# Seven quarter-product units of the second feed-forward layer placed anew, and the mLSTM's head steps later in TensorE's order

## The chip, the cores and the metric

One core of one Trainium2 chip runs the whole program. The metric is the device time of one execution in microseconds (us), the median of several runs. The core's engines are PE (TensorE, matmuls), DVE (VectorE), ACT (ScalarE), POOL (GpSimd) and SP (SyncE, which here only issues DMAs). Each has its own list of instructions, taken in order, and they wait for each other through semaphores.

## The reference, cut to what matters

Two layers over x of 256 positions by 2048 channels, float32. Layer 0 is pooling and attention, layer 1 an mLSTM, and behind each comes a gated MLP with 5632 hidden channels:

```python
for layer in range(DEPTH):
    h = rms_norm(x, norm_mix[layer])
    if layer % 2 == 0:
        ...  # pooling, attention, output projection
    else:
        mixed = mlstm_mixer(h, w_in_c[o], b_gate_c[o], h_norm_c[o], w_out_c[o])
    x = x + mixed
    x = x + conv_ffn(rms_norm(x, norm_ffn[layer]), w_up[layer], conv_w[layer], conv_b[layer], w_down[layer])
def conv_ffn(x, w_up, conv_w, conv_b, w_down):
    u = x @ w_up
    ...  # u: width-3 convolution over positions
    gate, val = jnp.split(u, 2, axis=-1)
    return (jax.nn.silu(gate) * val) @ w_down
```

The mLSTM has 8 heads of 256 channels: per head a 256 by 256 score matrix with a mask, exponential weights and a normaliser for each of the two directions, times the values; then a per-head norm, times a sigmoid gate, and an output projection.

## The kernel before, in words

**Weights.** All weights pass through one stream (class Stream) of chunks of 128 by 1024 numbers, 512 KB each. SP issues a chunk's load into one of 7 buffers w (8 in the feed-forward layers), ACT copies it rounded into the first half of a buffer hl (L167), DVE writes the remainder into its second half (L168), so that three passes of TensorE (high times high, high times low, low times high) stand for one exact product. There are 5 buffers hl (6 in the feed-forward layers), so ACT and DVE work at most that many chunks ahead of PE. PE, whose program order is written out by hand, reads a chunk in 12 matmuls of 512 columns (names mv, mo, op, dn), or 16 of 512 and 256 columns by turns (mq, mk, up).

**The feed-forward layer.** The hidden channels are 44 row tiles of 128, gate and value together, in six chunks of 4, 8, 8, 8, 8 and 8 (FCH, L33). A tile is either plain (function up, name up) or one of four that a unit makes. A unit (quads, names p1, p4, p5, p6) multiplies the four quadrants of two row blocks and two column blocks with seven products in place of eight. That takes sums of the weight quadrants. They are made beforehand and lie in DRAM, named G, one for each of a unit's eight pairs of blocks. When a unit's products are done, DVE adds them up into tiles c, PE turns these round (name tr, in finish, L1110), and ACT and DVE make the convolution, the SiLU and the product (tail), which end in g. The function down (dn) then multiplies g with the down weights, in the order of row tiles that DORDER (L34) gives. PE's interleaving is laid down by the table UNITS (L1272), each entry of which is (chunk, half of the chunk, first and last slot, kind), and by _ffn_plan (L1279), which deals the units' steps into slots between plain tiles and down products. Kind 1 reads three sums of a pair from DRAM, kind 2 reads two and lets DVE add the third as the chunk passes by (L155).

**How the sums are made.** A table (places, L1462 to L1468) gives for each pair the chunk of the stream at whose load its steps are issued. Written (at, 5) they go by DMA in four steps 5 loads apart: SP copies parts of the weights from DRAM to DRAM and POOL adds other parts to them with accumulating DMAs (L139, L143). Written (at, 1, 6) they go by DVE: SP loads the pair's 1 MB into a buffer in SBUF called a room (gb or gm, L120), DVE makes four additions of 128 by 512 (L124 to L127), and SP stores the result (L129). Rooms are handed out in the order of st.rooms (L772).

**The mLSTM.** For each pair of heads PE multiplies values (mv), then for each head queries and keys (mq, mk, 64 matmuls each), then the output gate of the pair (mo, 96 matmuls). Each head also runs a chain of small steps: qk (PE), the weighting and the matrix A (DVE), its transpose atr (PE), a copy and remainder at (ACT, DVE), the product with the values av (PE), a norm whose power -0.5 is taken on POOL (ry_h, L303), and, with the gate og (ACT and DVE, whose reciprocals stand at L923), the transpose htr (PE). These steps are generators in a list (class Weave). Each yields a delay in PE's microseconds, and the next one's PE instructions are put into PE's order when that many have been emitted. For PE's order the delays are thus the only thing that matters. DVE's, ACT's and SP's order is set by a scheduler that works on estimates of its own.

Of the kernel before, what the change touches and what calls it, by code (L numbers as in the profile page):

```python
# [32 lines left out]
FCH = [4, 8, 8, 8, 8, 8]  # L33
DORDER = ((0, 1), (0, 1, 3, 2), (2, 3, 0, 1), (0, 1, 3, 2), (0, 1, 3, 2), (0, 1, 3, 2))  # L34
CH = 8
# [213 lines left out]
def trunk(ctx: ExitStack, tc: tile.TileContext, gx, xT, xn, call, catt, cml, weights, make, out):  # L249
# [22 lines left out]
    st = Stream(tc, wp, sp, made, weights, make, 5, 2)  # L272
# [14 lines left out]
    wv = Weave()  # L287
# [473 lines left out]
    def mlstm_layer(norm, nxt):  # L761
        with ExitStack() as es:
# [7 lines left out]
            gm = kp.tile([P, 2048], F32, tag="gm", name="gm")  # L770
            gb = actp.tile([P, 2, 2048], F32, tag="B1", name="gb")
            st.rooms = ([gb[:, 0], gb[:, 1], gm] * 7)[:20] + [gm] * 8  # L772

# [13 lines left out]
            def gates(ps):  # L787
# [34 lines left out]
                a.dma_start(gd, gr)  # L822
                yield 16.0
                cols = psp.tile([P, 2, 2, 40], F32, tag="ps", name="cols")
                n = 0
# [28 lines left out]
            def head(h, q, kk, vt, hh):  # L854
# [10 lines left out]
                a.activation(arg, arg, AF.Exp)  # L865
                yield 5.5
                qk = psp.tile([P, 2, S], F32, tag="ps", name=f"qk{h}")
# [7 lines left out]
                for i, (t, d, c, n, o) in enumerate(blocks):  # L875
# [11 lines left out]
                                       ALU.mult, ALU.add)  # L887
                yield 5.0
                tr = psp.tile([P, 2, S], F32, tag="ps", name=f"atr{h}")
# [5 lines left out]
                v.tensor_sub(at[:, 1], tr, at[:, 0].bitcast(F32))  # L895
                yield 3.2
                av = psp.tile([P, 2, MD], F32, tag="ps", name=f"av{h}")
# [12 lines left out]
                for t in range(2):  # L910
                    a.activation(hn[:, t, :], av[:, t, :], AF.Copy, scale=r[:, t : t + 1])
                hns[h] = hn

            def gated(ps, heads):
                og = t1p.tile([P, 2, len(heads) * MD], F32, tag="og", name=f"og{heads[0]}")
                for t in range(2):
                    a.activation(og[:, t, :], ps[:, t, :], AF.Exp, scale=nrcol[:, t : t + 1])
                yield 1.2
                for i, h in enumerate(heads):
                    o = og[:, :, i * MD : i * MD + MD]  # L920
                    v.tensor_scalar_add(o, o, 1.0)
# [50 lines left out]
    def ffn_layer(layer, norm, nxt):  # L972
        with ExitStack() as es:
# [79 lines left out]
            def quads(fs, c, i0, name, apart):  # L1053
# [34 lines left out]
                for p in range(m):  # L1088
# [9 lines left out]
                    if p % 2:  # L1098
# [53 lines left out]
            def down(c, gt, b):  # L1152
                kts = [2 * k + j for k in DORDER[c] for j in range(2)]
                last = c == len(FCH) - 1
# [108 lines left out]
def _down_chunks(w):  # L1263
    out, k0 = [], 0
    for n in FCH:
# [10 lines left out]
)  # L1276


def _ffn_plan(layer):  # L1279

    slots = []
    for c, n in enumerate(FCH):
        fill = [("n", c, i) for i in range(n) if not any(u[0] == c and u[1] == i // 4 for u in UNITS[layer])]
        if c:
            per = len(fill) // NB
            fill = sum(([*fill[per * b : per * b + per], ("d", c - 1, b)] for b in range(NB)), [])
            if c == 2 and any(u[:2] == (1, 1) for u in UNITS[layer]):
                fill = [fill[i] for i in ((0, 2, 1, 4, 3, 6, 5, 7), (0, 1, 3, 2, 5, 7, 4, 6))[len(UNITS[layer]) > 6]]
            if c > 3 and len(UNITS[layer]) > 5:
                fill.sort(key=lambda e: e[0] == "d")  # L1290
        for e in fill:
# [31 lines left out]
def _ffn_order(layer, up, dn, four, last):  # L1323
# [4 lines left out]
    for step in _ffn_plan(layer):  # L1328
# [5 lines left out]
        elif kind == "d":  # L1334
            seq.append(dn[d0[c] + i * (FCH[c] // 2) + DORDER[c][n]])
        else:
# [141 lines left out]
```

## Time and profile before

| | us |
|---|---|
| median of 3 runs | 2164.73 (2164.2 to 2165.07) |
| the profiled execution, whole | 2164.91 |
| its span, first to last instruction | 2163.1 |
| PE busy | 2147.9 |
| DVE busy | 1798.1 |
| ACT busy | 1334.9 |
| POOL busy | 237.3 |

Layer 1's mLSTM lies between about 967 and 1454 us of the span, its feed-forward layer from there to the end. A matmul's duration in the profile holds its way through the array, so that those that follow each other overlap: PE counts as busy from a matmul's start until its modelled end, and only what is left beyond that shows as a wait.

### The profile page before, as it was taken

What the parts mean: (1) busy time and instruction counts of PE and PEld (TensorE: products, weight loads), DVE (VectorE), ACT (ScalarE), POOL (GpSimd) and SP (SyncE); (2) the same over time, 40 slices, a digit from 0 to 9 for tenths busy, and PEclk for the clock granted to TensorE, in tenths of its full rate; (3) what the DMA queues carried; (4) which work ended last, traced back from release to release, by engine and by line L of the source; (5) the groups of instructions that cost most, each with busy time, mean ns of one, the idle gap of its engine ahead of it and who ended that gap; (6) DMA issues with size and microseconds to landing.
All of it is one profiled execution on the core that took longest, in us unless ns stands there. A gap on an engine that the chain in (4) does not pass through costs nothing.

```text
span 2163.1 us, 30963 instructions
## 1 busy us (share of the span) xinstructions
PE 2147.9 (99%) x10752; PEld 1815.6 (84%) x10752; DVE 1798.1 (83%) x2522; ACT 1334.9 (62%) x1872; POOL 237.3 (11%) x296
## 2 busy tenths in 40 slices
PE   9999999999999999999999999999999999999999
PEld 7888888888888888888788888888888887888887
DVE  7686698989889888868888877769898888988985
ACT  7665566766557565755444544456685776766853
POOL 0222111111111111100000000000111111110000
PEclk9999999999999999999999999999999999999999
DMA  9889889999999999969898977778999999998882
GB/s 351 257 226 254 257 255 353 304 341 316 310 336 303 350 306 363 319 187 311 326 361 320 347 253 275 273 267 228 339 336 342 349 319 350 347 317 300 279 269 98
DMA packets 212768, 648.59 MB, mean 300 GB/s; under 512 B 26394, under 2 KB 28738, under 8 KB 205442
## 3 DMA queue, kind: packets, MB, share of 16 engines
q1 hardware_dynamic: 181216, 593.30, 76.4%
q0 software_dynamic: 28320, 49.56, 14.5%
q10 hardware_dynamic: 3074, 3.75, 0.8%
q8 instruction: 84, 1.38, 0.2%
q14 instruction: 74, 0.61, 0.1%
HBM read 615.00 MB, written 130.07 MB: 344 GB/s over the span
## 4 chain that ended last, share of the span: by engine, by line
PE 94%; DVE 3%; DMA 1%; issue 1%; ACT 1%; ACTq 0%; SPq 0%; DVEq 0%
PE dn L296 21%; PE p L296 20%; PE up L296 20%; PE op L296 8%; PE mo L296 3%; PE mv L296 3%; PE mk L296 3%; PE mq L296 3%; PE qproj L296 3%; DVE hl L168 2%; PE kproj L296 1%; PE pool L296 1%; PE vproj L296 1%; PE tr L1117 1%; DMA gb<-in_q 1%
## 5 line engine op out<-in xcount | busy, mean ns | idle before, releaser
L167 ACT CAST hl<-w 128x1024 fp32r<-128x1024 f32 (+2 forms) x915 | 947.5, 1048 | 616.0 <-PE dn L296 105.3
L168 DVE TENSOR_TENSOR hl<-w,hl 128x1024 fp32r<-128x1024 f32 (+1 forms) x916 | 1104.6, 1219 | 258.1 <-ACT hl L167 241.1
L296 PE MATMUL dn<-hl,g 128*128 128x512 f32 x2064 | 493.5, 391 | 1.9 <-DVE g L1001 1.6
L296 PE MATMUL up<-xx,hl 128*128 128x512 f32 (+1 forms) x2560 | 467.4, 337 | 0.0
L296 PEld LDWEIGHTS up<-xx,hl 128*128 128x128 f32 x2560 | 405.8, 188 | 64.0
L296 PEld LDWEIGHTS dn<-hl,g 128*128 128x128 f32 x2064 | 385.0, 188 | 82.5 <-DVE g L1001 2.5
L296 PE MATMUL p<-hl,sx 128*128 128x512 f32 x1152 | 305.3, 390 | 1.1 <-DVE hl L168 1.1
L296 PEld LDWEIGHTS p<-hl,sx 128*128 128x128 f32 x1152 | 212.2, 188 | 43.2 <-DVE hl L168 1.6
L296 PE MATMUL p<-hl,xx 128*128 128x512 f32 x864 | 236.4, 391 | 0.0
L296 PEld LDWEIGHTS p<-hl,xx 128*128 128x128 f32 x864 | 158.1, 188 | 30.1
L139 POOL DMA_DIRECT2D G<-in_q x136 | 114.2, 842 | 626.8 <-DMA G<-in_q 623.1
L143 POOL DMA_DIRECT2D G<-G x120 | 102.0, 850 | 561.6 <-DMA G<-in_q 218.1
L296 PE MATMUL mk<-xx,hl 128*128 128x512 f32 (+1 forms) x512 | 92.2, 338 | 0.0
L296 PE MATMUL mq<-xx,hl 128*128 128x512 f32 (+1 forms) x512 | 92.2, 337 | 0.0
L296 PE MATMUL mo<-hl,xx 128*128 128x512 f32 x384 | 92.1, 396 | 0.0
L296 PE MATMUL mv<-hl,xx 128*128 128x512 f32 (+2 forms) x480 | 91.7, 350 | 0.0
L296 PE MATMUL op<-hl,cat 128*128 128x512 f32 x384 | 91.6, 393 | 0.0
L296 PE MATMUL op<-hl,mcat 128*128 128x512 f32 x384 | 89.5, 392 | 0.0
L296 PEld LDWEIGHTS mq<-xx,hl 128*128 128x128 f32 x512 | 79.3, 188 | 11.6
L296 PEld LDWEIGHTS mk<-xx,hl 128*128 128x128 f32 x512 | 79.0, 188 | 11.4
L296 PEld LDWEIGHTS mv<-hl,xx 128*128 128x128 f32 x480 | 78.3, 189 | 11.2
L296 PEld LDWEIGHTS mo<-hl,xx 128*128 128x128 f32 x384 | 72.1, 191 | 14.7
(250 smaller groups left out, 1947.6 us busy)
## 6 DMA issues: line engine op xcount, KB each, us to landing
w<-in_dn SPq DMA_DIRECT2D x176, 512.0 KB, 7.6
w<-in_up SPq DMA_DIRECT2D x160, 512.0 KB, 7.2
w<-in_m_in SPq DMA_DIRECT2D x124, 512.0 KB, 6.5
w<-G SPq DMA_DIRECT2D x88, 512.0 KB, 8.3
w<-in_q SPq DMA_DIRECT2D x80, 512.0 KB, 7.4
G<-in_q SPq DMA_DIRECT2D x120, 256.0 KB, 7.5
G<-G POOLq DMA_DIRECT2D x120, 256.0 KB, 7.6
w<-in_q SPq DMA_DIRECT2D x120, 256.0 KB, 7.0
```

The costliest lines, as they stand in the source:

```text
L139: pin(add.dma_start(G[r, 0:512], src[r, 512:1024], accum_op=ALU.add))
L143: pin(add.dma_start(G[:, at : at + 512], G[:, of : of + 512], accum_op=ALU.add))
L167: (self.nc.vector.tensor_copy if i + c == 0 else self.nc.scalar.copy)(hl[:, 0, c : c + n], w[:, c : c + n])
L168: self.nc.vector.tensor_sub(hl[:, 1, c : c + n], w[:, c : c + n], hl[:, 0, c : c + n].bitcast(F32))
L296: pe.matmul(out_, lhsT, rhs, start=start, stop=stop, skip_group_check=True)
L1117: pe.transpose(tr[:, j, t * P : t * P + P], src[:, c : c + P], ident)
```

## The change

**Of the units.** There are seven units in the second feed-forward layer before and after. Before they are (1,1), (2,1), (3,0), (3,1), (4,0), (4,1), (5,1), now (1,1), (2,0), (2,1), (3,1), (4,0), (4,1), (5,1): chunk 2 is made of units alone, and four tiles of chunk 3 are plain that were a unit's. Three units are of kind 1 and four of kind 2 before and after. The instructions of PE, ACT and DVE are the same in number and shape but for eight additions (L124 to L127, two pairs) that DVE no longer makes. These two pairs now go by DMA: SP has two loads and two stores of rooms fewer and eight copies more, POOL eight accumulating DMAs more. Where the sums are made changes more: of the 56 pairs, 26 go by DVE (28 before), all in the mLSTM; 30 go by DMA, 7 of them in the first feed-forward layer as before, 7 in the last 64 chunks of the mLSTM (none before), and 16 in the feed-forward layer itself (21 before).

**Of the mLSTM.** The delays between the steps of a head grow, and so do those of the gates' columns (cols) and of htr.

**Of both feed-forward layers.** DORDER is one order for all chunks, which alters chunk 2 alone, and the first two transposes of a unit come 1.5 us later in PE's order.

```diff
-DORDER = ((0, 1), (0, 1, 3, 2), (2, 3, 0, 1), (0, 1, 3, 2), (0, 1, 3, 2), (0, 1, 3, 2))
+DORDER = (0, 1, 3, 2)
-            st.rooms = ([gb[:, 0], gb[:, 1], gm] * 7)[:20] + [gm] * 8
+            st.rooms = [gb[:, 0], gb[:, 1], gm] * 6 + [gm] * 8
@@ gates: ahead of cols
-                yield 16.0
+                yield 18.5
@@ head: ahead of qk, of atr, of av
-                yield 5.5
+                yield 7.5
-                yield 5.0
+                yield 8.0
-                yield 3.2
+                yield 4.0
@@ head: ahead of the gate's product
+                yield 6.0
                 hns[h] = hn
@@ gated: ahead of htr
-                    yield 4.5
+                    yield 5.5
@@ quads
-                            wv.add(finish(c12, c22, fs[2:], gt, i0 + 2, name), 3.0)
+                            wv.add(finish(c12, c22, fs[2:], gt, i0 + 2, name), 4.5)
@@ UNITS, second layer
-    ((1, 1, 16, 33, 2), (2, 1, 34.5, 50.5, 1), (3, 0, 51.5, 67, 1), (3, 1, 68, 83, 1), (4, 0, 84, 98.5, 2),
+    ((1, 1, 16, 33, 1), (2, 0, 34, 50, 2), (2, 1, 51, 66.5, 1), (3, 1, 67.5, 82, 2), (4, 0, 83, 97.5, 2),
@@ kernel: places of the second layer's pairs
-    places.append([(at - 240 + 11 * k, 5) for k in range(7)]
-                  + [(at - 152 + 17 * k // 4, 1, 6) for k in range(20)] + [(at - 63 + 8 * k, 1, 5) for k in range(8)]
-                  + [(at + 12 * k, 5) for k in range(21)])
+    early = [(at - 240 + 11 * k, 5) for k in range(7)]
+    late = [(at - 64 + 9 * k, 4) for k in range(7)]
+    here = [(at + 8 + 14 * k, 5) for k in range(16)]
+    vec = [(at - 146 + 9 * k // 2, 1, 6) for k in range(18)] + [(at - 60 + 7 * k, 1, 5) for k in range(8)]
+    places.append(vec[:8] + early + vec[16:17] + vec[8:16] + late + vec[17:18] + here + vec[18:])
```

Three places of the order. First PE in the mLSTM, at head 1: the rows between its scores (qk1) and the transpose of its matrix A (atr1), the first rows of before, the second of the change. A row's last number is how many such matmuls follow each other.

```order
L296 MATMUL qk1_9901<-hl_k1_9832,hl_q1_9697 128x256 x12
L296 MATMUL mo0_9835<-hl433_9842,xx2_2493 128x512 x12
L296 MATMUL mo0_9835<-hl434_9869,xx2_2493 128x512 x12
L892 MATMUL atr1_9968<-cst_87,A1_9923 128x128 x4
L296 MATMUL mo0_9835<-hl435_9886,xx2_2493 128x512 x12
```

```order
L296 MATMUL qk1_9911<-hl_k1_9795,hl_q1_9688 128x256 x12
L296 MATMUL mo0_9798<-hl434_9855,xx2_2493 128x512 x12
L296 MATMUL mo0_9798<-hl435_9874,xx2_2493 128x512 x12
L296 MATMUL mo0_9798<-hl436_9896,xx2_2493 128x512 x12
L296 MATMUL mo0_9798<-hl437_9940,xx2_2493 128x512 x6
L892 MATMUL atr1_10006<-cst_87,A1_9933 128x128 x4
```

Between the two stood 24 matmuls of mo, and now stand 42. It is the same for the other odd heads. For the even ones (qk0 to atr0 and so on) 24 of mq and 8 of mk have become 12 and 40. Ahead of qk0 stood 40 of mq1, now 52; ahead of cols 60 of mq0, now 64 and 12 of mk0.

Second, DVE in the second feed-forward layer: the rows from the first sum on plain tile 37 (tb_up1_37, which must wait until PE has ended that tile) to the split of weight chunk 845 (hl845), which PE needs for unit (4,1). Again before, then after.

```order
L461 TENSOR_TENSOR tb_up1_37_18328<-up1_37_18172,tb_up1_37_18328 128x512
L1011 TENSOR_TENSOR tb_up1_37_18328<-tb_up1_37_18328,R3_13465 128x512
L168 TENSOR_TENSOR hl844_18345<-w844_18262,hl844_18345 128x1024
L155 TENSOR_TENSOR w845_18284<-w845_18284 128x512
L168 TENSOR_TENSOR hl846_18370<-w846_18295,hl846_18370 128x1024
L168 TENSOR_TENSOR hl847_18382<-w847_18306,hl847_18382 128x1024
L993 SCALAR_TENSOR_TENSOR y1_37_18332<-tb_up1_37_18328,cst_87,y1_37_18332 128x255 x2
L168 TENSOR_TENSOR hl848_18404<-w848_18343,hl848_18404 128x1024
L995 SCALAR_TENSOR_TENSOR y1_37_18332<-tb_up1_37_18328,cst_87,y1_37_18332 128x255
L168 TENSOR_TENSOR hl845_18358<-w845_18284,hl845_18358 128x1024
```

```order
L461 TENSOR_TENSOR tb_up1_37_18356<-up1_37_18176,tb_up1_37_18356 128x512
L168 TENSOR_TENSOR hl847_18386<-w847_18311,hl847_18386 128x1024
L168 TENSOR_TENSOR hl848_18398<-w848_18322,hl848_18398 128x1024
L1012 TENSOR_TENSOR tb_up1_37_18356<-tb_up1_37_18356,R3_13510 128x512
L168 TENSOR_TENSOR hl845_18337<-w845_18278,hl845_18337 128x1024
```

Eleven instructions have become five.

Third, POOL at the end of the mLSTM, the powers of heads 5 to 7 (ry_h5 to ry_h7) and of the norm ahead of the feed-forward layer (ry_n3), all of before, then a piece of the change around head 6. G131 and G140 are pairs of units (3,1) and (4,0).

```order
L303 TENSOR_TENSOR ry_h5_11765<-rv_h5_11763,mhalf_118 128x2
L303 TENSOR_TENSOR ry_h6_12369<-rv_h6_12367,mhalf_118 128x2
L303 TENSOR_TENSOR ry_h7_12615<-rv_h7_12613,mhalf_118 128x2
L139 DMA G140_3_13218<-in_q1 64x512 x2
L303 TENSOR_TENSOR ry_n3_13418<-rv_n3_13416,mhalf_118 128x2
```

```order
L143 DMA G131_1_11853<-G131_1_11853 128x512
L139 DMA G131_2_12076<-in_q1 64x512
L143 DMA G131_2_12076<-G131_2_12076 128x512
L139 DMA G131_3_12339<-in_q1 64x512
L143 DMA G131_2_12076<-G131_2_12076 128x512
L303 TENSOR_TENSOR ry_h6_12452<-rv_h6_12450,mhalf_118 128x2
L139 DMA G131_3_12339<-in_q1 64x512
L143 DMA G131_3_12339<-G131_3_12339 128x512
```

No accumulating DMA stood between the heads' powers, and now they stand among them from head 5 on.

More of the change, by code (lines that the diff above doesn't have):

```diff
@@ L1152, in down @@
             def down(c, gt, b):
-                kts = [2 * k + j for k in DORDER[c] for j in range(2)]
+                kts = [2 * k + j for k in DORDER[: FCH[c] // 2] for j in range(2)]
                 last = c == len(FCH) - 1
@@ L1286, in _ffn_plan @@
             fill = sum(([*fill[per * b : per * b + per], ("d", c - 1, b)] for b in range(NB)), [])
[L1287 to L1290, printed above, removed]
+            if c == 2 and any(u[:2] == (1, 1) for u in UNITS[layer]) and len(fill) > 4:
+                fill = [fill[i] for i in (0, 2, 1, 4, 3, 6, 5, 7)]
+            if len(UNITS[layer]) > 6:
+                fill = [fill[i] for i in (0, 1, 2, 3, 4, 6, 5, 7)] if c == 1 else sorted(fill, key=lambda e: e[0] == "d")
         for e in fill:
@@ L1334, in _ffn_order @@
         elif kind == "d":
-            seq.append(dn[d0[c] + i * (FCH[c] // 2) + DORDER[c][n]])
+            seq.append(dn[d0[c] + i * (FCH[c] // 2) + DORDER[n]])
         else:
```

2 rows, old and new, of the table UNITS are left out of this document.

## Prediction

> **What bounds the kernel now.** The page first: its span, PE's line, and the row of the commonest matmul.
>
> ```profile
> span 2163.1 us, 30963 instructions
> ...
> PE 2147.9 (99%) x10752; PEld 1815.6 (84%) x10752; DVE 1798.1 (83%) x2522; ACT 1334.9 (62%) x1872; POOL 237.3 (11%) x296
> ...
> L296 PE MATMUL dn<-hl,g 128*128 128x512 f32 x2064 | 493.5, 391 | 1.9 <-DVE g L1001 1.6
> ```
>
> PE is busy 2147.9 of 2163.1 us, so all that a change of order can win lies in 15 us of idle time and in whatever slows PE while it counts as busy. A matmul of 512 columns lasts 391 ns, but the next starts about 0.23 us after it (24 take 5.63 us below), so 0.16 us of every lost moment is hidden inside a busy one. The waits of PE come next (total, number, longest).
>
> ```profile
> PE atr L892 <- DVE A L884: 4.5, 3, 3.2
> PE dn L296 <- DVE g L1001: 1.6, 2, 1.1
> PE wps L320 <- DVE pad L689: 1.2, 1, 1.2
> PE p L296 <- DVE hl L168: 1.1, 1, 1.1
> PE tr L1117 <- DVE c L1094: 1.0, 1, 1.0
> PE qk L296 <- DVE hl_k L843: 0.7, 1, 0.7
> PE cols L296 <- ACT rows_b L819: 0.5, 1, 0.5
> PE qk L296 <- ACT hl_k L842: 0.4, 1, 0.4
> ```
>
> The same view over stretches of the span puts atr, qk and cols into the mLSTM and dn, p and tr into the second feed-forward layer; the wait of wps is the program's start. Then the longest of them, in PE's order of time:
>
> ```profile
> 1053.56 5.63 PE L296 MATMUL mo<-hl,xx 128*128 128x512 f32 x24
> 1062.38 0.66 PE L892 MATMUL atr<-cst,A 128*128 128x128 f32 x4 [3.18 <-DVE A L884]
> 1062.79 5.96 PE L296 MATMUL mo<-hl,xx 128*128 128x512 f32 x18
> 1068.59 1.59 PE L296 MATMUL av<-mvt,at 128*128 128x256 f32 x12
> 1070.02 4.27 PE L296 MATMUL mo<-hl,xx 128*128 128x512 f32 x18
> ```
>
> After the 24 matmuls of mo PE stands 3.18 us until DVE has finished A. Then 18 matmuls of mo take 5.96 us, where the next 18 take 4.27: 1.7 us more. The clock column (the figure behind POOL's busy time) says why:
>
> ```profile
> 1058.00:1062.00 4.00, 1.20 (x6) 0.66 (x4) 3.41 (x8) 1.04 (x1) 0.00 (x0) 1.00 0.97 360
> 1063.00:1067.00 4.00, 4.00 (x13) 3.11 (x12) 1.63 (x4) 1.43 (x2) 0.00 (x0) 0.57 1.01 420
> 1067.00:1071.00 4.00, 4.00 (x25) 3.53 (x24) 2.43 (x3) 1.83 (x5) 0.00 (x0) 1.00 0.79 182
> ```
>
> After the wait the granted clock falls to 0.57 over four microseconds, and is full again behind them. The last question is what DVE does where PE waits for it (busy PE, PEld, DVE, ACT, POOL, then clock, share of the DMA engines, GB/s):
>
> ```profile
> 1000.00:1050.00 50.00, 48.41 (x278) 41.98 (x277) 46.48 (x86) 27.14 (x37) 1.02 (x1) 1.00 0.97 352
> 2000.00:2050.00 50.00, 48.87 (x253) 41.19 (x252) 48.84 (x71) 41.60 (x61) 0.00 (x0) 1.00 0.85 275
> ```
>
> DVE is busy 46.5 and 48.8 of 50 us there, and 83% over the whole. PE is the bound, and where DVE's work bunches DVE becomes it for a microsecond or three. Except for cols and one qk, which wait for ACT, each wait above is for DVE.
>
> **The change, part by part.** PE's work is the same, with seven units in both, so nothing is won by fewer matmuls. The whole effect is in waits.
>
> *Removed in the mLSTM.* Between qk1 and atr1 stand 18 more matmuls of mo, 18 times 0.23 = 4.1 us, against a wait of 3.2; DVE's steps between the two grow by nothing. The other two waits of atr (4.5 − 3.2 = 1.3 us together) get the same 4.1. An mk matmul takes 0.177:
>
> ```profile
> 1107.96 11.31 PE L296 MATMUL mk<-xx,hl 128*128 128x512 f32 x64
> ```
>
> Ahead of qk0 stand 12 more of mq, 2.1 us against 0.7 and 0.4, and ahead of cols 16 more, 2.8 against 0.5. What is late next in each chain is later on PE too: av follows atr by 24 matmuls of mk and 6 of mo where it was 20 of mk, and htr moves behind six more of mv and av itself. Removed are 4.5 + 0.7 + 0.4 + 0.5 = 6.1 us, and 6 times 0.16 = 1.0 hidden ones, and the half clock's 1.7, as no wait of its length is left. Together 8.8.
>
> [...]
>
> *Removed in the second feed-forward layer.* Four waits, 1.6 + 1.1 + 1.0 = 3.7 us, with 4 times 0.16 = 0.6 hidden: 4.3. They are due to how DVE's instructions fall between PE's, and both are dealt anew. So I counted: for each PE instruction that waits for DVE, the PE work since the instruction that last let DVE go on, against DVE's instructions between the two. The second place of the order is an example. These are rows of DVE and PE there before:
>
> ```profile
> 2000.11 0.69 DVE L155 TENSOR_TENSOR w<-w 128x512 f32<-128x512 f32 x1
> ...
> 2000.71 2.35 DVE L168 TENSOR_TENSOR hl<-w,hl 128x1024 fp32r<-128x1024 f32 x2
> ...
> 2002.98 0.88 DVE L993 SCALAR_TENSOR_TENSOR y<-tb_up,cst,y 128x255 f32<-128x255 f32 x2
> ...
> 2004.91 0.48 DVE L995 SCALAR_TENSOR_TENSOR y<-tb_up,cst,y 128x255 f32<-128x255 f32 x1
> ...
> 2005.31 1.22 DVE L168 TENSOR_TENSOR hl<-w,hl 128x1024 fp32r<-128x1024 f32 x1
> ...
> 2006.58 1.45 PE L296 MATMUL p<-hl,sx 128*128 128x512 f32 x5 [1.13 <-DVE hl L168]
> ```
>
> Two splits take 2.35 us and one 1.22, so one follows another after 1.14; likewise a sum of 512 takes 0.60 (from 2000.11 to 2000.71) and a convolution step 0.40 (two 0.88, one 0.48). Before, the eleven instructions come to 5 × 1.14 + 3 × 0.60 + 3 × 0.40 = 8.7 us, and with 1.4 for ACT's copy and the semaphores (a value that fits these waits) 10.1. PE has 37 products for it, 8.5 us: 1.6 short, and it waited 1.13 and a hidden 0.16. Now five instructions make 3 × 1.14 + 2 × 0.60 + 1.4 = 6.0 against 25 products, 5.7: 0.3 short. The same count at all other places of before gives 3.3 for atr1, 0.6 and 0.7 for atr5 and atr7, 1.1 for tr, 1.6 and 1.0 for dn, close to what PE waited, and nothing elsewhere; it misses qk0 and cols.
>
> *Added.* In the changed order that count falls short at five places only: htr0 by 0.4, atr4 by 0.7 (DVE meets the sum of tb_q5, which must await mq5's end, ahead of A), tr of unit (1,1) by 0.1, hl845 by 0.3, and tr of unit (4,1) by 0.6 on top of that. Sum 2.1. For what it does not see I add 0.7, as it missed 1.6 of 9.8 us before. Bounds of all this: none, and as much as the 4.3 of the layer before.
>
> *Moved off DVE and onto POOL and the DMA engines.* Eight additions fewer save DVE 5 us of its 1798, on no path. But seven pairs go by DMA in the last 64 chunks of the mLSTM. Prices from the page:
>
> ```profile
> q1 hardware_dynamic: 181216, 593.30, 76.4%
> q0 software_dynamic: 28320, 49.56, 14.5%
> ...
> L139 POOL DMA_DIRECT2D G<-in_q x136 | 114.2, 842 | 626.8 <-DMA G<-in_q 623.1
> L143 POOL DMA_DIRECT2D G<-G x120 | 102.0, 850 | 561.6 <-DMA G<-in_q 218.1
> ```
>
> 593.3 MB in 76.4% of 2163 us are 2.79 us of all engines for 1 MB; POOL's 260 DMAs in 14.5% are 1.2 us each. The 64 chunks of 0.524 MB take 94 us, eight pairs by DVE at 2.1 MB each way summed take 47, and a pair by DMA 0.79 MB (2.2 us) and four accumulating ones (4.8), seven of them 49. That is 190 us of transfers in 64 × 2.78 = 178 of PE, where before it was 141:
>
> ```profile
> 1350.00:1400.00 50.00, 49.22 (x229) 40.71 (x228) 37.28 (x51) 22.76 (x31) 0.69 (x1) 1.00 0.77 271
> 1400.00:1450.00 50.00, 50.00 (x234) 41.41 (x233) 34.08 (x43) 28.52 (x43) 1.65 (x2) 1.00 0.80 273
> 1600.00:1650.00 50.00, 50.00 (x246) 42.18 (x245) 44.82 (x61) 37.31 (x51) 6.51 (x8) 1.00 1.02 335
> 1650.00:1700.00 50.00, 50.00 (x242) 41.87 (x241) 43.99 (x57) 35.85 (x46) 7.28 (x9) 1.00 1.03 342
> ```
>
> The first two rows show that stage at 0.77 and 0.80 before. The last two show the feed-forward layer, which runs at 1.02 and 1.03 without one wait of PE for a transfer. 190 of 178 is 1.07, so about 7 us of transfers are late at the end, against the three split chunks (3 × 2.78 = 8.3 us) that I take the stream to keep ahead of PE in the mLSTM, where it has 5 buffers hl and PE holds one or two. I take nothing for it; uncovered it would cost 7, or at most the 12 by which 190 exceeds 178. [...]
>
> *The sum.* 2164.9 for the profiled execution − 8.8 − 4.3 + 2.1 + 0.7 = 2154.6. The median of before is 0.2 lower, so 2154.4.
>
> **The rivals.** *The feed-forward layer keeps its waits* (0.14). DVE is as full there as before, and the count is finer than the estimates by which the scheduler put DVE's rows. With 4.3 in place of the 1.0 counted there: 2157.7. *The half clock stays*, because something other than this wait brings it, or because a new wait near 3 us does (0.05): 2154.4 + 1.7 = 2156.1. [...] *Late transfers show* (0.09): 2161 with 7 us, 2166 with 12, for which 1.07 speaks, and against it the cover. *The delays do nothing* (0.03), because DVE's scheduler has moved A and the rest back by as much: only the layer's gain is left, 2164.7 − 3.3 + 0.7 = 2162.1. The rows of the order speak against it.
>
> *Slower: POOL holds up the heads* (0.05). POOL takes its list in order, and the powers ry_h6, ry_h7 and ry_n3 now stand behind accumulating DMAs, each of which waits for a copy. Before, nothing held them for long:
>
> ```profile
> 1332.24 1.00 POOL L303 TENSOR_TENSOR ry_h<-rv_h,mhalf 128x2 f32<-128x2 f32 x1 [67.76 <-DVE rv_h L301]
> 1360.59 0.69 POOL L303 TENSOR_TENSOR ry_h<-rv_h,mhalf 128x2 f32<-128x2 f32 x1 [27.35 <-DVE rv_h L301]
> 1457.38 0.71 POOL L303 TENSOR_TENSOR ry_n<-rv_n,mhalf 128x2 f32<-128x2 f32 x1 [11.39 <-DVE rv_n L301]
> ```
>
> In the feed-forward layer such a DMA waited up to 14.0 us:
>
> ```profile
> POOL G L139 <- DMA G<-in_q: 256.1, 39, 14.0
> ```
>
> DVE, in order too, then stands at the norm's next step and its splits with it. It decides once the hold exceeds the 8.3 us of split chunks ahead. With 14.0 at heads 5, 6, 7 and the norm that is 4 × 5.7 = 23 us: 2177. Against it: 7 buffers w and 5 hl let SP issue the copies up to twelve chunks, 33 us, before PE is at the chunk of their place.
>
> **How the numbers follow.** The forecast keeps 0.64. A measurement of this kernel can tell 0.2%, 4.3 us, from no change, so faster is below 2160.4: the forecast, the kept waits, the half clock and the mildest third of the late transfers, 0.64 + 0.14 + 0.05 + 0.03 = 0.86. Within: 0.06 + 0.03 = 0.09. Slower: 0.05. The range goes from 2151.5, where all 13.1 us are removed and nothing is added, to 2160.5. It leaves out most of the late transfers, the idle delays, POOL's hold and a little for what I have not thought of, 0.16.
>
> **What would show it.** Right: no wait of qk, cols, nor of atr over 1 us, a granted clock of 1.00 from 1050 to 1100, under 1.5 us of waits in the second feed-forward layer, PE's busy time 1 to 3 us lower. Wrong: a wait of PE on hl in the mLSTM's end with ACT waiting for w (transfers), or DVE waiting for ry_h or ry_n (POOL); a wait of htr, the chain's last step, over 2 us, or of tr and dn over 1 us.

## The result and the profile after

The changed kernel takes 2151.62 us (median of 4, 2151.58 to 2151.8) where the kernel before took 2164.9 in the same session (4 runs, 2164.2 to 2166.14). The ratio is 0.9938, with an interval of 0.9921 to 0.9955. That is 13.3 us less, where 10.3 were forecast. The median lies 0.1 us above the low end of the range; the ratio times the 2164.73 on which the range was built is 2151.3, 0.2 below it. The sign was right, the size was 3 us too small, and, as the runs show, the larger half of it came by another way than the prediction said.

The page of the profiled execution (2151.58 us, span 2149.8), first its span, PE's line and the commonest matmul:

```profile
span 2149.8 us, 30986 instructions
...
PE 2143.8 (100%) x10752; PEld 1813.8 (84%) x10752; DVE 1792.6 (83%) x2514; ACT 1335.6 (62%) x1872; POOL 243.6 (11%) x304
...
L296 PE MATMUL dn<-hl,g 128*128 128x512 f32 x2064 | 491.5, 391 | 0.0
```

PE's busy time fell by 4.1 us and its idle time by 9.2. All waits of PE (total, number, longest):

```profile
PE wps L320 <- DVE pad L689: 1.2, 1, 1.2
PE htr L933 <- DVE hn L928: 0.3, 1, 0.3
PE kproj L296 <- ACT xx L359: 0.3, 1, 0.3
PE tr L1118 <- DVE c L1095: 0.3, 1, 0.3
PE p L296 <- DVE hl L168: 0.2, 1, 0.2
```

Of the eight rows before, five are gone: atr, dn, both rows of qk, and cols. The wait of p is 0.2 for 1.1, that of tr 0.3 for 1.0, and htr is new with 0.3, as is kproj in layer 0. The stretches that the prediction had quoted (busy PE, PEld, DVE, ACT, POOL, then clock, share of the DMA engines, GB/s):

```profile
1000.00:1050.00 50.00, 50.00 (x288) 43.62 (x287) 46.60 (x85) 27.11 (x37) 0.71 (x1) 1.00 0.91 350
1050.00:1100.00 50.00, 49.66 (x250) 41.80 (x249) 43.47 (x69) 25.92 (x34) 0.69 (x1) 1.00 0.89 328
1350.00:1400.00 50.00, 50.00 (x233) 41.58 (x232) 36.52 (x45) 23.57 (x34) 5.58 (x7) 1.00 0.97 312
1400.00:1450.00 50.00, 50.00 (x241) 41.62 (x240) 34.11 (x46) 29.01 (x45) 5.60 (x7) 1.00 0.93 321
2000.00:2050.00 50.00, 49.73 (x250) 41.84 (x249) 48.28 (x71) 40.34 (x59) 0.00 (x0) 1.00 0.85 283
```

The clock between 1050 and 1100 is 1.00 instead of 0.97, so the half clock is gone. DVE is as full as before, 46.6 and 48.3 of 50 us. The end of the mLSTM now runs its DMA engines at 0.97 and 0.93, and PE waits for no transfer there.

For what follows I cut each trace at three matmul starts: the first mv, the last op, the last dn. The first stretch is the mLSTM, the second the feed-forward layer behind it.

| kernel | time | mLSTM | feed-forward |
|---|---|---|---|
| before | 2164.9 | 486.8 | 693.9 |
| after | 2151.6 | 478.5 | 689.3 |
| before, new delays | 2164.4 | 485.7 | 693.9 |
| before, new places and rooms | 2160.5 | 480.7 | 694.0 |
| after, old delays | 2153.0 | 479.7 | 689.2 |
| after, old places and rooms | 2164.1 | 486.7 | 694.5 |
| after, DVE's sums one chunk later | 2164.9 | 491.7 | 689.2 |
| before, DVE's sums eight chunks later | 2158.0 | 479.7 | 693.9 |
| after, two delays more | 2150.7 | 478.0 | 688.9 |

Times are medians, of several sessions; stretches are from each kernel's one trace. The feed-forward stretch repeats to some tenths where nothing in it was changed. The mLSTM's does not where a half clock lies in it: the kernel before with the later finish alone, whose mLSTM is the old one, has 488.2, with a granted clock of 0.50 for 6.83 us in it where the kernel before has it for 3.41. The trace of the new places and rooms alone is of a run of 2158.8 us, below that kernel's median. Of the 13.3 us, 8.3 were won in the mLSTM, 4.6 to 4.7 in the feed-forward layer, and 0.4 outside both.

### The profile page after: what moved, and what is told of

It reads as the page before. It is cut to its first block, busy times and chain, and to the rows that moved or that the text cites. A ratio compares the mean times of both kernels' runs of the same rounds, so it can differ in the third digit from the quotient of the medians.

```text
span 2149.8 us, 30986 instructions
## 1 busy us (share of the span) xinstructions
PE 2143.8 (100%) x10752; PEld 1813.8 (84%) x10752; DVE 1792.6 (83%) x2514; ACT 1335.6 (62%) x1872; POOL 243.6 (11%) x304
## 4 chain that ended last, share of the span: by engine, by line
PE 97%; DVE 2%; issue 0%; DMA 0%; ACT 0%; ACTq 0%; DVEq 0%
PE dn L296 22%; PE p L296 21%; PE up L296 20%; PE op L296 8%; PE mk L296 4%; PE mq L296 4%; PE mo L296 4%; PE mv L296 4%; PE qproj L296 3%; PE kproj L296 1%; PE pool L296 1%; PE vproj L296 1%; PE tr L1118 1%; DVE hl L168 1%; PE qk L296 1%; PE end L296 1%
## 5 line engine op out<-in xcount | busy, mean ns | idle before, releaser
L143 POOL DMA_DIRECT2D G<-G x124 | 108.2, 872 | 550.8 <-DMA G<-in_q 231.2
L296 PEld LDWEIGHTS op<-hl,mcat 128*128 128x128 f32 x384 | 71.4, 188 | 14.6
```

The lines of the kernel that those rows point to most:

```text
L143: pin(add.dma_start(G[:, at : at + 512], G[:, of : of + 512], accum_op=ALU.add))
L296: pe.matmul(out_, lhsT, rhs, start=start, stop=stop, skip_group_check=True)
```

## The experiments

The theory on record had two parts: the new delays empty the mLSTM of waits, and the new units do it in the feed-forward layer. The rival is that it is DVE's list, in which the additions for the weight sums (L124 to L127) stand between the steps of a head, that makes the waits, so that the places of the sums decide. With the new units goes an edit of _ffn_plan that the diff above does not show: in the second layer the lists of plain tiles and down products of chunks 1, 2 and 3 are put in another order. No run parts it from the table UNITS.

**One delay alone.** Kernel before:

```diff
-                yield 5.0
+                yield 8.0 if h == 1 else 5.0
                 tr = psp.tile([P, 2, S], F32, tag="ps", name=f"atr{h}")
```

> The kernel before with one delay changed: the one ahead of atr, 5.0 to 8.0, for head 1 alone. The theory of the prediction (the delay removes the wait, and the wait brings the half clock): the wait of atr1 (3.18 us, 3.34 between starts) goes, and with it the 1.7 us of the half clock, against a new shortfall of 0.3 at head 2's scores: 2164.9 - 3.3 - 1.7 + 0.3 = 2160.2 us. If the half clock is not this wait's: 2161.9. If the order of DVE moves back by as much: 2164.9.

It took 2160.67 us, ratio 0.9979 (0.997 to 0.9989). The wait of atr1 and the fall of the clock are gone (1.00 from 1050 to 1100 us), so a longer delay can remove such a wait, and the fall was that wait's. The new wait at head 2's scores did not come. The waits that were left came out longer in this trace, the other two of atr 1.7 us for 1.3 and that of the scores of head 0 for ACT 1.0 for 0.4, so the gain is 4.5 us against the 5.0 of the wait and the fall.

**All delays alone**, in the kernel before, everything else old:

```diff
-                yield 16.0
+                yield 18.5
...
-                yield 5.5
+                yield 7.5
...
-                yield 5.0
+                yield 8.0
...
-                yield 3.2
+                yield 4.0
...
+                yield 6.0
                 hns[h] = hn
...
-                    yield 4.5
+                    yield 5.5
```

> The kernel before with all the new delays of the mLSTM and nothing else. Theory of the prediction's second term (the delays remove the mLSTM's waits, 8.8 us with the half clock, and leave 0.5 at the first htr): 2164.9 - 8.3 = 2156.6. Theory that an order of DVE decides each wait, and that the old places of the sums give it another order under the same delays: counted from the built program, DVE is 4.8 us late at the first htr and 0.4 at that of head 6; such a wait brings a half clock of its own (1.7 or more): 2164.9 - 8.8 + 5.2 + 1.7 = 2163.0, and without a half clock 2161.3.

It took 2164.43, ratio 0.9998 (0.9989 to 1.0007): nothing. All its waits of PE:

```profile
PE htr L933 <- DVE hn L928: 5.5, 3, 4.6
PE dn L296 <- DVE g L1002: 1.6, 2, 1.1
PE wps L320 <- DVE pad L689: 1.2, 1, 1.2
PE p L296 <- DVE hl L168: 1.1, 1, 1.1
PE tr L1118 <- DVE c L1095: 1.0, 1, 1.0
```

Every wait of atr, qk and cols is gone, as the prediction said of the delays, and htr takes their place with 5.5 us, 4.6 of them at head 0, with a granted clock of 0.57 from 1087 to 1091 us, behind that wait. "htr, the chain's last step, over 2 us" stood among the prediction's signs of error. It was right to fear it, but it had counted htr0 with the new places, where it is short by only 0.4.

**The changed kernel with the old delays** (the edit above, turned round):

> The changed kernel with the six delays of the mLSTM put back; units, places and rooms, DORDER and the finish stay. If the delays alone remove the mLSTM's waits, only the feed-forward layer's gain is left, 4.7 us by the trace after: 2160.2 us. If DVE's order decides, the new places alone take away the waits of atr1, atr5 and atr7 with the half clock (6.6 us), since the count finds no shortfall over 0.3 us there in this kernel, and only cols and qk0 (2.2 us) stay: 2164.9 - 6.6 + 0.2 - 4.7 = 2153.8.

It took 2152.98, ratio 0.9945 (0.993 to 0.996). The mLSTM's waits stay away without the delays, those of qk and cols too, which the count cannot see. Why atr1 no longer waits is told by DVE's list between the scores of head 1 and its A. This is before, and after there stands none of the lines marked with a minus:

```
 L876 arg1<-qk1,arg1 128x128
 L876 arg1<-qk1,arg1 128x256 x2
 L876 arg1<-qk1,arg1 128x128
-L127 gm<-gm 128x512
-L126 gb<-gb 128x512
 L879 denr1<-den1 128x4
-L168 hl438<-w438,hl438 128x1024
-L127 gb<-gb 128x512
 L880 denr1<-denr1,mc 128x4
 L881 denr1<-denr1 128x4
-L168 hl439<-w439,hl439 128x1024
 L883 A1<-arg1,denr1 128x256
 ...
 L886 A1<-arg1,denr1,A1 128x128
```

Three additions for sums and two splits stood ahead of A, and by the count the second split waits until PE has let a buffer go, near the end of the mo ahead of atr1. The same five are missing in the changed kernel with the old delays, and in the one with the new delays alone. Either edit takes this wait away; the sum of the two is not the sum of their gains. What the old delays leave, beside 0.2 us at htr of head 0, is one wait of 1.3 us at htr of head 6. The timeline of DVE ahead of it:

```profile
1366.08 0.69 DVE L124 TENSOR_TENSOR gm<-gm 128x512 f32<-128x512 f32 x1 [1.61 <-DMA gm<-in_q]
1366.69 2.35 DVE L168 TENSOR_TENSOR hl<-w,hl 128x1024 fp32r<-128x1024 f32 x2
1368.96 0.68 DVE L927 TENSOR_TENSOR hn<-hn,og 128x512 f32<-128x512 f32 x1
```

DVE, in order, stood 1.61 us for the load of a room (gm<-in_q) ahead of the product that htr needs. The delays are worth this wait and little else: 2152.98 against 2151.62.

**The places alone, and the units without the places.** The kernel before with this edit, and the changed kernel with the same edit turned round:

```diff
-    places.append([(at - 240 + 11 * k, 5) for k in range(7)]
-                  + [(at - 152 + 17 * k // 4, 1, 6) for k in range(20)] + [(at - 63 + 8 * k, 1, 5) for k in range(8)]
-                  + [(at + 12 * k, 5) for k in range(21)])
+    early = [(at - 240 + 11 * k, 5) for k in range(7)]
+    late = [(at - 64 + 9 * k, 4) for k in range(7)]
+    here = [(at + 8 + 14 * k, 5) for k in range(16)]
+    vec = [(at - 146 + 9 * k // 2, 1, 6) for k in range(18)] + [(at - 60 + 7 * k, 1, 5) for k in range(8)]
+    places.append(vec[:8] + early + vec[16:17] + vec[8:16] + late + vec[17:18] + here + vec[18:])
...
-            st.rooms = ([gb[:, 0], gb[:, 1], gm] * 7)[:20] + [gm] * 8
+            st.rooms = [gb[:, 0], gb[:, 1], gm] * 6 + [gm] * 8
```

> The kernel before with the new places of the sums and the new order of rooms alone; units, finish, DORDER and delays are the old ones. If the places decide the mLSTM, its waits are those of the changed kernel with the old delays (htr 0.4 and 1.5 us), 7 us less than before with the half clock, and the feed-forward layer keeps its five waits (5.0 us between starts): 2153.0 + 4.7 = 2157.7. If the places make the feed-forward layer's gain too: 2153.0. If they make nothing without the new units: 2164.9.

> The changed kernel with the old places of the sums and the old order of rooms; the new units, finish, DORDER and mLSTM delays stay. If the places decide DVE's order in the mLSTM, its waits are those of the run with the delays alone (htr 4.8 and 1.2 us, and a half clock), and the feed-forward layer keeps the gain of the new units (by count only 0.1 and 0.3 us of waits there): 2164.4 - 4.7 + 0.0 = 2159.7. If the units alone make all the difference: 2151.6. If the places make the feed-forward layer's gain too: 2164.4.

The places alone: 2160.5, ratio 0.9978 (0.9969 to 0.9987). Most of the mLSTM's gain is theirs, 486.8 to 480.7 us. Two waits of the scores came up at head 6 that no count had shown (0.9 and 0.7 us), and the expected 1.5 at htr did not come. The traced run took 2158.8, 1.1 over the expected 2157.7. The single runs are of two kinds: four with a granted clock of 1.000 took 2157.9 to 2159.0, six with 0.999 took 2160.4 to 2161.5. The feed-forward layer keeps every wait it had: 694.0 us. The changed kernel without the places: 2164.07, ratio 0.9995 (0.9986 to 1.0004), in place of the 2159.7 expected. The mLSTM is that of the delays alone, as expected. But the feed-forward layer gained nothing, 694.5 us, although its tr and dn<-g waits are gone. Others have come (waits of PE in this kernel):

```profile
PE htr L933 <- DVE hn L928: 5.9, 3, 4.6
PE p L296 <- DVE hl L168: 2.8, 3, 1.8
```

ACT's waits for transfers between 1800 and 1930 us, of which the changed kernel has none there:

```profile
ACT hl L167 <- DMA w<-G: 10.4, 10, 2.9
ACT hl L167 <- DMA w<-in_dn: 7.5, 8, 2.3
ACT hl L167 <- DMA w<-in_b: 6.5, 3, 2.9
```

PE now waits for splits of weights, and ACT ahead of them for transfers of weights and sums (w<-G, w<-in_dn, w<-in_b). So the layer's gain needs both edits: with the new units the waits for DVE go, and with the new places these waits for transfers stay away. Why they do was not told apart. The share of the DMA engines between 1800 and 1850 us is 1.03 here, 1.03 before and 1.02 after. With the old places 21 pairs are summed by DMA in the layer itself, with the new ones 16; but the kernel before has those 21 too, and in the same stretch its ACT waits 3.9 us for transfers, not 24, and its PE for no split. What only this kernel has is that the old places give the pairs of units (1,1) and (5,1), now of kind 1, to the DMA. Such a pair takes two accumulating DMAs of 64 by 1024 (L134): there are 30 of them here and none before or after. From 1454 to 2148 us the two large queues moved 213 MB in this kernel, 209 before and 201 after. The new places alone give kind 1 to the DMA as well (28 such DMAs), all ahead of this layer.

**One chunk.** Here vec and the second list of the old places are the pairs that DVE adds up. If the places act through DVE's order, then their phase should decide, not their number. Changed kernel, then kernel before:

```diff
-    vec = [(at - 146 + 9 * k // 2, 1, 6) for k in range(18)] + [(at - 60 + 7 * k, 1, 5) for k in range(8)]
+    vec = [(at - 145 + 9 * k // 2, 1, 6) for k in range(18)] + [(at - 60 + 7 * k, 1, 5) for k in range(8)]
...
-                  + [(at - 152 + 17 * k // 4, 1, 6) for k in range(20)] + [(at - 63 + 8 * k, 1, 5) for k in range(8)]
+                  + [(at - 144 + 17 * k // 4, 1, 6) for k in range(20)] + [(at - 63 + 8 * k, 1, 5) for k in range(8)]
```

> The changed kernel with one number changed: DVE's 18 pairs begin one chunk later, at - 145 + 4.5 k for at - 146 + 4.5 k. If the phase of the sums against the heads decides DVE's order, this one chunk gives back what the change won in the mLSTM: by count DVE is 4.8 us late at htr of head 0 and 4.2 at that of head 2, each over the length at which the clock fell: 2151.6 + 4.8 + 4.2 - 0.5 + 2 x 1.7 = 2163.5, within 1 us of no gain at all. If the number or the kind of the sums matters and not their phase: 2151.6.

> The kernel before with one number changed: DVE's 20 pairs begin 8 chunks later, at - 144 + 4.25 k for at - 152 + 4.25 k. If the phase decides, atr1's 3.3 us shrink to 0.6 by count and the half clock goes with it, atr5's 0.7 go too, and atr7, the scores and cols stay as they are: 2164.9 - 2.8 - 0.7 - 1.7 = 2159.7. If the phase does not matter: 2164.9.

The first took 2164.92, ratio 1.0001 (0.9992 to 1.001): one number, one chunk, and the whole gain is gone. That the time is just that of before is chance: the feed-forward layer keeps its gain, and the mLSTM is 4.9 us longer than before. Its waits of htr, and then the window behind the first, with the clock ahead of the last two columns:

```profile
PE htr L933 <- DVE hn L928: 8.6, 2, 4.6
```

```profile
1084.61:1091.44 6.83, 4.89 (x14) 4.03 (x15) 2.95 (x5) 1.99 (x3) 0.00 (x0) 0.50 0.97 396
```

The clock is half for 6.83 us there, and for as long again from 1187.01 on, behind the second. That is twice the length of the fall before, and why the time is 1.4 us over the expected 2163.5.

The timeline of DVE ahead of htr0, some rows, first the shifted kernel:

```profile
1075.39 0.68 DVE L127 TENSOR_TENSOR gm<-gm 128x512 f32<-128x512 f32 x1
...
1077.40 0.68 DVE L124 TENSOR_TENSOR gb<-gb 128x512 f32<-128x512 f32 x1
...
1080.86 1.74 DVE L924 RECIPROCAL og<-og 128x256 f32<-128x256 f32 x1
...
1084.20 1.75 DVE L924 RECIPROCAL og<-og 128x256 f32<-128x256 f32 x1
1085.86 0.63 DVE L928 TENSOR_TENSOR hn<-hn,og 128x512 f32<-128x512 f32 x1
```

and the changed one:

```profile
1074.62 0.69 DVE L124 TENSOR_TENSOR gb<-gb 128x512 f32<-128x512 f32 x1
...
1078.01 0.69 DVE L127 TENSOR_TENSOR gb<-gb 128x512 f32<-128x512 f32 x1
...
1078.69 1.75 DVE L924 RECIPROCAL og<-og 128x256 f32<-128x256 f32 x1
...
1081.43 0.68 DVE L928 TENSOR_TENSOR hn<-hn,og 128x512 f32<-128x512 f32 x1
```

From the first step of the gate on DVE (L922, at 1066.8 and 1066.7 us) to hn, the shifted kernel has seven additions for two pairs (gm, then gb), all four reciprocals of the gate and six splits; the changed one has four additions for one pair, three reciprocals and five splits. The product hn comes at 1085.86 instead of 1081.43. The second kernel, the one before with one number changed, took 2157.95, ratio 0.997 (0.9959 to 0.9981): half of the gain of the whole change. Its waits of atr are two, 0.5 and 0.9, and those of qk and cols, which I had left in, are not in its trace.

**How long a wait lowers the clock.** Changed kernel with further work on DVE ahead of atr, which leaves A as it was:

```diff
+                for _ in range({1: 4, 3: 6, 5: 8, 7: 18}.get(h, 0)):
+                    tc.keep_in_program_order(v.tensor_scalar_mul(A[:, 1, :], A[:, 1, :], 1.0))
```

> The changed kernel with 4, 6, 8 and 18 further multiplications by one of half of A (128 by 256 each) on DVE ahead of atr of heads 1, 3, 5, 7, so that the result is the same. By count PE then waits about 2.6, 3.1, 3.7 and 4.5 us for A at the four heads. If a wait of about 3.2 us brings the half clock, as it seemed to before, the granted clock falls behind the second or third, third and fourth, for some 4 us each, and not behind the first. If the half clock before had another cause, it falls behind none. [...] Time: 2151.6 + 14 us of waits + 1.7 for each fall, 2168 to 2172.

It took 2170.65 us (one run). The four waits in the timeline of PE:

```profile
1066.10 0.55 PE L894 MATMUL atr<-cst,A 128*128 128x128 f32 x3 [2.30 <-DVE A L889]
...
1165.61 0.55 PE L894 MATMUL atr<-cst,A 128*128 128x128 f32 x3 [2.95 <-DVE A L889]
...
1266.81 0.90 PE L894 MATMUL atr<-cst,A 128*128 128x128 f32 x3 [3.62 <-DVE A L889]
...
1369.43 0.90 PE L894 MATMUL atr<-cst,A 128*128 128x128 f32 x3 [5.08 <-DVE A L889]
```

and the windows of 4 us behind each:

```profile
1066.00:1070.00 4.00, 3.90 (x19) 3.29 (x20) 1.36 (x4) 2.51 (x4) 0.00 (x0) 1.00 0.92 334
1165.00:1169.00 4.00, 3.39 (x16) 2.84 (x17) 1.32 (x4) 2.00 (x4) 0.00 (x0) 1.00 0.97 275
1266.00:1270.00 4.00, 3.19 (x9) 2.69 (x10) 1.37 (x4) 0.58 (x1) 0.00 (x0) 0.58 1.02 375
1369.00:1373.00 4.00, 3.57 (x11) 3.00 (x12) 1.03 (x3) 0.80 (x2) 0.00 (x0) 0.57 0.90 306
```

After 2.30 and 2.95 us the clock stays full, after 3.62 and 5.08 it is half for 3.41 us. Before it fell after 3.18. Counted from the end of the columns of the matmul ahead, which the profile's wait leaves out (0.16 to 0.20 us here), these five are 2.50, 3.15, 3.34, 3.82 and 5.28. That looks like a length, between 3.15 and 3.34, at which the fall begins, but more than the length decides. The same wait of 3.18 us, at the same place, stands in the kernel before and in the kernel with the later finish (next experiment). These windows are cut where the clock changes, first in the kernel before, then in the other:

```profile
1060.08:1063.49 3.41, 1.11 (x7) 1.03 (x8) 3.15 (x8) 0.62 (x2) 0.00 (x0) 1.00 1.01 422
1063.49:1066.91 3.42, 3.42 (x10) 2.66 (x9) 1.14 (x3) 1.01 (x2) 0.00 (x0) 0.50 1.02 428
```

```profile
1058.23:1061.64 3.41, 0.97 (x5) 0.47 (x3) 2.83 (x6) 1.04 (x1) 0.00 (x0) 1.00 0.97 370
1061.64:1068.47 6.83, 6.08 (x17) 4.93 (x18) 3.05 (x9) 1.37 (x2) 0.00 (x0) 0.50 0.97 392
```

PE waits until 1062.38 in both. In the first the clock falls 1.1 us after the wait's end, for 3.41 us; in the second 0.7 us ahead of it, for 6.83, and the 18 matmuls of mo behind it take 6.85 us where they took 5.96. In every trace the clock changes only at whole multiples of 3.413 us from its first rise in that trace. From the matmuls' starts I worked out the share of each stretch of that length in which PE's columns stood idle. The ten stretches behind which the clock fell, ahead of the program's end, were idle for 0.65 to 1.0 (0.74 and 0.77 in the two above, 1.0 twice in the ladder). No stretch that the full clock outlived was idle for more than 0.6. The wait of 2.95 lies across a border and makes 0.52 and 0.47. So in these traces it counted beside a wait's length how the wait lay to these stretches.

**The finish alone, and the late pairs packed.** The kernel before with the unit's first transposes 1.5 us later (3.0 to 4.5), and the changed kernel with this:

```diff
-    late = [(at - 64 + 9 * k, 4) for k in range(7)]
+    late = [(at - 32 + 4 * k, 4) for k in range(7)]
```

> The kernel before with one number changed: the delay of a unit's first transposes, 3.0 to 4.5, in both feed-forward layers. Alone it removes the wait of tr at unit (1,1), 1.0 us (1.19 between starts); the count from the built program finds a new shortfall of 1.0 us at the split of weight chunk 888. Count: 2164.9 - 1.2 + 1.0 = 2164.7. If the new shortfall doesn't come: 2163.7.

> The changed kernel with the seven late pairs of DMA sums packed into the last 32 chunks of the mLSTM (from at - 32, 4 apart) in place of the last 64. The instructions on PE, DVE and ACT stay. By the prediction's prices these 32 chunks then ask for 47 us of weights, 23 of DVE's pairs and 49 of the late ones, 119 in 89 us of PE: with 8.3 us of cover the rest shows, 2151.6 + 22 = 2174, and POOL's powers wait behind the accumulating DMAs. If transfers and POOL have as much room as the run after suggests (DMA share 0.92 to 0.98 there and no wait): 2151.6 to 2155.

The finish gave 2165.43, ratio 1.0001 (0.9992 to 1.001). Its wait of tr is gone, and p waits twice for a split where it had waited once, as counted:

```profile
PE p L296 <- DVE hl L168: 2.1, 2, 1.1
```

The packed pairs took 2158.39 (one run), 6.8 us more, a third of what the prediction's prices make of it. The timeline of DVE there, then the row of ACT's waits and that of PE's:

```profile
1429.83 1.22 DVE L168 TENSOR_TENSOR hl<-w,hl 128x1024 fp32r<-128x1024 f32 x1 [5.22 <-ACT hl L167]
1430.97 1.28 DVE L470 TENSOR_TENSOR x<-x,op 128x512 f32<-128x512 f32 x2
```

```profile
ACT hl L167 <- DMA w<-in_m_out: 19.1, 8, 5.4
```

```profile
PE xt L347 <- DVE x L470: 4.4, 1, 4.4
```

Transfers are late now, and the DMA engines' share between 1400 and 1450 us is 1.03. PE does not miss the chunk itself but xt: DVE's list has a split ahead of the residual x, the split waits 5.22 us for ACT, ACT up to 5.4 us for the chunk's transfer, and PE for x. Whether SP or the DMA engines held the transfer was not told apart. The clock is half from 1429.32 us on, for 6.83. On POOL the power of the last head and that of the norm wait for DVE alone; those of the heads ahead come before the packed DMAs, so for them this run shows nothing.

**Better than both.** Two tries at the three small waits that are left (htr0, hl845, tr of unit (4,1)):

```diff
-                    yield 5.5
+                    yield 6.5 if h == 0 else 5.5
...
-     (4, 1, 98.5, 113, 2), (5, 1, 114, 127.5, 1)),
+     (4, 1, 98.5, 113.5, 2), (5, 1, 114, 127.5, 1)),
```

> The changed kernel with two numbers more: the delay ahead of htr of head 0 from 5.5 to 6.5, and the last slot of unit (4,1) from 113 to 113.5. By count the three waits that are left (htr0 0.50 us, hl845 0.39, tr of unit (4,1) 0.48, between starts) go and nothing comes: 2151.6 - 1.4 = 2150.2. If DVE's order only moves them elsewhere: 2151.6.

It took 2155.5, ratio 0.9955 (0.9943 to 0.9967), 3.9 us more than the changed kernel. The three waits are gone, and there is one that the count could not see, since it looks at DVE alone (timeline of ACT and PE):

```profile
2026.51 0.59 ACT L1120 COPY tb<-tr 128x512 f32<-128x512 f32 x1 [0.39 <-DVE y L996]
...
2027.15 1.19 PE L296 MATMUL p<-hl,xx 128*128 128x512 f32 x3 [3.46 <-ACT tb L1120]
```

A product waits for ACT's copy of a transpose to free its accumulator, and that copy stands in ACT's list behind steps of y that wait for DVE. The wait brought a half clock of 3.41 us with it. So the slots were left alone and the transposes moved by 0.5 us:

```diff
-                            wv.add(finish(c12, c22, fs[2:], gt, i0 + 2, name), 4.5)
+                            wv.add(finish(c12, c22, fs[2:], gt, i0 + 2, name),
+                                   5.0 if layer and fs[0] == 32 else 4.5)
```

> The changed kernel with the delay ahead of htr of head 0 from 5.5 to 6.5, as before, but with the units' slots left alone; instead the first transposes of unit (4,1) come 0.5 us later (4.5 to 5.0). By count htr0's 0.50 us go, and all but about 0.1 of the 0.48 us of tr; hl845's 0.39 stay: 2151.6 - 0.9 = 2150.7. If ACT's copies wait in their turn as in the run before: 2154 to 2156.

It took 2150.73 (2150.66 to 2151.09), ratio 0.9938 (0.9926 to 0.9951), 0.9 us less than the changed kernel, as expected, and the fastest of all. The two were timed in different sessions and have the same ratio; that the 0.9 is real rests on the two traces, whose stretches differ by as much. PE's waits are 1.2 us at the program's start and 0.2 at hl845.

## Why the prediction was right and wrong, point by point

- **"Between qk1 and atr1 stand 18 more matmuls of mo … DVE's steps between the two grow by nothing."** This is the step that failed: it puts the mLSTM's removed waits down to the new delays, with DVE's list taken as it was. In the changed kernel DVE's rows there shrink from fifteen to ten, and with this list the wait is gone under the old delays too. In the mLSTM the delays alone win 1.1 us, since DVE is then 4.6 late at htr0, the places and rooms alone 6.1, both 8.3. The reason given was possible, as the run with head 1's delay shows, but it does not carry the gain. That the size of what is removed came out right (8.8, less the 0.5 left at htr0, are the 8.3 measured) is luck: the same waits go in either way.
- **"Eight additions fewer save DVE 5 us of its 1798, on no path."** The count of additions is on no path, as said. Their places are: moved by one chunk they cost 13.3 us.
- **"The delays do nothing", 0.03.** This rival had the right doubt and a wrong consequence. The delays do little, but the mLSTM's waits go all the same, so 2162.1 was never near.
- **The half clock.** The 1.7 us were won, as forecast. With head 1's delay alone the wait and the fall go together, so the fall was this wait's and the rival is out. Its price in that trace was that of one stretch of 3.413 us. With the later finish the same wait of 3.18 us brought two, and by my estimate from the granted clock (1.000 in 13 of 64 runs) some runs of the kernel before had none. The stretch ahead of the fall was idle for 0.74 of it.
- **The feed-forward layer, 4.3 removed and 1.0 left.** Measured: 4.6 to 4.7 gained with 0.9 left (hl845 0.39 for 0.3, tr of unit (4,1) 0.48 for 0.6, tr of unit (1,1) none for 0.1), so 5.5 removed. The count of what is left was good to 0.1 us. What was removed was taken 1.2 too small, and this is the term that was mis-sized most: the waits come to 5.0 between starts, where I had 3.7 and 0.16 for each of four; the last 0.5 I cannot place.
- **Added in the mLSTM, 0.4 and 0.7.** htr0 was 0.5. At atr4 the wait was under 0.1, since PE's mk matmuls ahead of it took about 0.2 us longer than my values, and DVE's way to A about 0.4 less.
- **0.7 for what the count doesn't see.** It did not come in the changed kernel. In the run with the slots moved it came fivefold, through ACT. This point, the two ahead of it and the 0.4 us outside both stretches are the 3 us by which the forecast was too high.
- **Transfers at 1.07.** They came to 0.92 to 0.98, and nothing is late. From the windows the seven pairs took about 36 us of the DMA engines, not 49.
- **"PE's busy time 1 to 3 us lower."** It is 4.1 lower. The prediction's own 1.7, 1.0 and 0.6 already make 3.3 of that.
- **POOL holds up the heads, 0.05.** It does not. In the changed kernel's timeline of POOL the powers of heads 5 to 7 and that of the norm wait only for DVE:

```profile
1361.41 0.71 POOL L303 TENSOR_TENSOR ry_h<-rv_h,mhalf 128x2 f32<-128x2 f32 x1 [11.85 <-DVE rv_h L301]
...
1446.86 0.79 POOL L139 DMA_DIRECT2D G<-in_q  x1 [17.01 <-DMA G<-in_q]
1448.97 0.71 POOL L303 TENSOR_TENSOR ry_n<-rv_n,mhalf 128x2 f32<-128x2 f32 x1 [1.33 <-DVE rv_n L301]
```

For the norm it was close. The accumulating DMA just ahead of its power waited 17.0 us for its copy, more than the 14.0 that the prediction feared, and POOL was free again 1.3 us before DVE's value came.

- **The range.** Its low end was the sum with all removed and nothing added (2164.7 − 13.1 is 2151.6; it was set at 2151.5). That bounds the additions, but not the removals, which had an error of their own (1.2 us in one layer).

## What to carry to other kernels

Where engines take their lists in order, a wait belongs to what stands ahead in the list: look at the rows between an input's arrival and the waited step, on both kernels, before a removed wait is put down to the edit that is easiest to see. Background work on the same engine, the same in amount, cost 13.3 us here when it was moved by one chunk, so its phase against the critical steps is a parameter to scan, and two edits that each remove the same wait do not add. A count of work between two engines, made from the built lists, finds such waits to a few tenths of a microsecond, but it has to take in every engine of the chain.

## What the runs showed of the hardware

TensorE's granted clock changed, in every trace here, only at whole multiples of 3.413 us from its first rise, and each fall to a half ahead of the program's end lasted one or two such stretches (3.41 us in five falls, 6.83 in five). By the shares worked out from the matmuls' starts, the ten stretches ahead of these falls were idle for 0.65 to 1.0, and none that the full clock outlived was for more than 0.6. A wait of 3.18 us brought one stretch at half clock in one trace and two in another. The shift by one chunk made 8.9 us of waits between starts and two falls of 6.83 us, and that kernel took 13.3 us longer in all.

The spread of some kernels' single runs goes with this. The kernel before ran 64 times in the three sessions of the experiments, from 2162.46 to 2169.74 us. The median is 2163.2 for the 13 runs with a granted clock of 1.000, 2164.7 for the 31 with 0.999 and 2166.2 for the 20 with 0.998. A stretch at half clock is 0.0008 of the span, so by my estimate these runs had none, one and two. Kernels without such waits spread by 0.2 to 0.5 us (2151.58 to 2151.8 after, 2157.7 to 2158.13 for the kernel before with the shifted sums). A spread is left within each group, 2163.5 to 2165.6 for the 31, and the waits of the scores for ACT differ from trace to trace (0.4, 0.7 and 1.0 us at head 0). What varies in them was not tried.
